# A two-layer encoder on one core: the second head pair's values in seven products, all values through memory, heads in four turns a chunk, and small moves at both ends

## The chip, the core and the metric

The kernel runs on one core of one Trainium2 chip. The metric is device time in microseconds (us) of one execution. Before the change three runs took 1619.01, 1621.74 and 1623.58 us, median 1621.74. The profiled execution, from which all rows below come, took 1620.87 us, of which the profile's span is 1619.1; the 1.8 us between them lie around the span.

## What is computed

The input is x, 512 tokens of width 2048 in float32. Two layers are added to it, each after an RMS norm, and a last RMS norm follows.

```python
def reference(x, norm_gain, final_gain, ...):
    for layer in range(2):
        hn = rmsnorm(x, norm_gain[layer])
        out = even_layer(hn, ...) if layer % 2 == 0 else odd_layer(hn, ...)
        x = x + out
    return rmsnorm(x, final_gain)

def odd_layer(h, w_in, gate_bias, norm_gain, w_out):
    proj = h @ w_in
    q, k, v, o, z, gates = split_at(proj, [1024, 1024, 2048, 2048, 2048, 32])
    # eight heads: q, k of 128 columns, v of 256; a forward and a backward mLSTM over chunks of 128 tokens
    h_f = mlstm_chunkwise(q, k, v, i_f, log_sigmoid(f_f))
    h_b = flip(mlstm_chunkwise(flip(q), flip(k), flip(v), flip(i_b), flip(log_sigmoid(f_b))))
    hs = rmsnorm(sigmoid(o) * (h_f + h_b), norm_gain)      # per head
    return (hs * silu(z)) @ w_out
```

The even layer is an attention of eight heads with two key and value heads beside a gated linear recurrence (RG-LRU), again between two large projections. The change lies in the odd layer, in the first chunk of the even layer's first projection, and in the final norm.

## The kernel before, in words

**Numbers.** Every float32 operand is split into a high and a low part (`split`, L152: ScalarE casts the high part, VectorE subtracts it to get the low one), and every product is made of three: high·high, high·low, low·high (`mm3`, L170). All matmuls are issued at L157, so rows of the profile are told apart by the names of the tiles.

**Bulk work.** The projections are a list of groups, each a block of weight columns in eight chunks of 256 rows, worked off by `run_steps` (L298). SP loads the chunk's weights (tile `raw`), `ahead` splits them early (`wh`, `wl`). There are two kinds of groups. A plain group has 512 columns in four PSUM banks and makes 192 matmuls of 512 moving columns (tile `bk`). A seven-product group adds and subtracts blocks of operands first (GpSimd sums weights into `w7s` and inputs into `ts`), so that seven block products do the work of eight; its matmuls have 256 moving columns (tile `s`). `run_w7c` works such a group of 512 columns: 8 chunks by 2 by 7 by 3, that is 336 matmuls. `run_w7` works one of 256 columns.

**Order of the odd layer.** Queries and keys; then `SC`, five seven-product groups of 512 columns: the values of head pair 0 (V0) and the gates O0 to O3; then the plain groups V1, V2, V3, Z3 and `out2` (the first 512 output columns); then five seven-product groups of 256 output columns (`u7`); then `run_last`, the last 256 output columns and the final norm.

**Heads.** The eight heads of the mLSTM (four pairs of two) and the transposition of their results (`hT_gen`) are generators in two lanes. While a plain group runs, lane 0 gets a turn after each bank listed in `TURNS`, so head work lies between bulk matmuls. `drain_until` runs a lane to its end where something later needs it: `h_split(c)`, which fetches the input chunk c of the output projection, needs that chunk stored by `hT_gen` (store to `hTd`, reload as `hTr`; the last pair's two chunks stay on chip as `hT`). A framework then orders each engine's instructions by their priorities and their dependences.

**Values.** V0 is scaled, stored to memory (`vd`) and reloaded (`vr`) by `v_gen`. V1 to V3 go straight from PSUM into the split tile `vv` (`v_evac`, L1174), which first drains the pair before (`need_h`).

**Both ends.** In the first chunk ScalarE writes the scaled high part `xh` (L527). At the end `acc` collects the squares of the output rows; `late_rows` (L1400) and `out2_square` (L1427) add to it, partly on GpSimd. `run_last` (L1439) makes two rows of blocks (`rows`), then two blocks of columns (`columns(0)`, `columns(1)`), each over 16 values of k. `next(between)` puts the row sums (`stc`, a matmul of ones with `acc`) and the spread reciprocal root (`rB`) among the columns' matmuls, at k = 1 and k = 5.

## Time and profile before

| What | us |
|---|---|
| runs, median (lowest to highest) | 1621.74 (1619.01 to 1623.58) |
| profiled execution, its span | 1620.87, 1619.1 |
| TensorE matmuls busy | 1598.5 (99% of the span) |
| VectorE, ScalarE, GpSimd busy | 1172.1, 881.8, 802.7 (72%, 54%, 50%) |
| five `SC` groups (963.70 to 1164.80) | 201.10 |
| last matmul to the end of the span | about 7 |

A timeline row gives start, duration, engine, line, operation, output and inputs, and in brackets the idle time of the engine ahead of it with what ended it. PE is TensorE, DVE is VectorE, ACT is ScalarE, POOL is GpSimd. [...] A row of a window gives the window, its length, the busy time of each engine with its count of instructions, the mean clock granted to TensorE (1.00 is full), the busy share of the DMA engines and their rate.

### The profile page before, as it was taken

To read this page: it belongs to the slowest core of one execution; us is meant where nothing else is said; L and a number is where in the kernel's file an instruction comes from. 1 tells how busy PE (TensorE), PEld (TensorE's weight loads), DVE (VectorE), ACT (ScalarE), POOL (GpSimd) and SP (SyncE) were. 2 spreads that over 40 slices of the span, in tenths; PEclk is the share of its full clock that TensorE was granted. 3 is DMA by queue.
4 is the path that set the end of the run, shared out by engine and by line. 5 is a ranking of instruction groups with operands and counts; after the bars stand their busy time and mean duration, and the time that the engine had idled before them with its cause. 6 is when DMAs were issued, how large, how long until landed. Compare 5 with 4: busy or idle time off the path is not lost.

```text
span 1619.1 us, 26278 instructions
## 1 busy us (share of the span) xinstructions
PE 1598.5 (99%) x9986; PEld 1431.9 (88%) x9986; DVE 1172.1 (72%) x1802; ACT 881.8 (54%) x1470; POOL 802.7 (50%) x804
## 2 busy tenths in 40 slices
PE   9999999999999999999999999999999999999997
PEld 7888888887888998889999999999988888888996
DVE  8755476766678786558998886666676676678875
ACT  6334666569584345544444444444566566565453
POOL 5220101101028884686787788888521322468862
PEclk9999999999999999999999999999999999999998
DMA  6533132431436358934444444444554344442564
GB/s 229 188 91 102 55 111 85 131 104 50 146 104 238 114 143 250 301 111 128 128 115 135 131 131 134 120 149 134 183 168 130 109 157 152 154 159 92 137 188 162
DMA packets 145486, 228.66 MB, mean 141 GB/s; under 512 B 10112, under 2 KB 70912, under 8 KB 145296
## 3 DMA queue, kind: packets, MB, share of 16 engines
q1 hardware_dynamic: 142000, 222.19, 43.6%
q0 software_dynamic: 2176, 4.19, 1.7%
q8 instruction: 78, 1.28, 0.3%
q10 hardware_dynamic: 1184, 0.60, 0.1%
q14 instruction: 48, 0.39, 0.1%
HBM read 189.17 MB, written 39.88 MB: 141 GB/s over the span
## 4 chain that ended last, share of the span: by engine, by line
PE 86%; DVE 4%; ACT 4%; POOL 2%; issue 2%; DMA 2%; SPq 0%; DVEq 0%; ACTq 0%; POOLq 0%
PE bk L157 41%; PE s L157 34%; DVE wl L154 2%; PE nf L157 2%; PE nb L157 2%; PE lg L157 1%; PE PV L157 1%; PE ST L157 1%; PE S L157 1%; PE tr L160 1%; ACT wh L153 1%; PE gt L157 0%; DMA hTr<-hTd 0%; DMA xres<-x2d 0%; DMA raw<-in_odd_w_out_dram 0%
## 5 line engine op out<-in xcount | busy, mean ns | idle before, releaser
L154 DVE TENSOR_TENSOR wl<-raw,wh 128x384 fp32r<-128x384 f32 (+3 forms) x349 | 365.4, 1049 | 185.0 <-ACT wh L153 184.3
L153 ACT CAST wh<-raw 128x384 fp32r<-128x384 f32 (+3 forms) x349 | 265.0, 762 | 378.8 <-PE s L157 274.9
L364 POOL TENSOR_TENSOR w7s<-raw 128x256 f32<-128x256 f32 x248 | 252.0, 1035 | 107.2 <-DMA raw<-in_odd_w_in_dram 61.4
L154 DVE TENSOR_TENSOR wl<-w7s,wh 128x512 fp32r<-128x512 f32 (+1 forms) x208 | 237.1, 1140 | 4.4 <-ACT wh L153 4.3
L157 PE MATMUL s<-th,wl 128*128 128x256 f32 x672 | 190.2, 283 | 0.8 <-DVE wl L154 0.8
L157 PE MATMUL s<-th,wh 128*128 128x256 f32 x672 | 189.1, 281 | 0.5 <-ACT wh L153 0.5
L157 PE MATMUL s<-tl,wh 128*128 128x256 f32 x672 | 189.2, 282 | 0.0
L157 PE MATMUL bk<-xh,wh 128*128 128x512 f32 x384 | 151.8, 395 | 0.0
L153 ACT CAST wh<-w7s 128x512 fp32r<-128x512 f32 (+1 forms) x208 | 145.3, 699 | 11.1 <-POOL w7s L364 9.5
L157 PE MATMUL bk<-xl,wh 128*128 128x512 f32 x384 | 151.3, 394 | 0.0
L157 PE MATMUL bk<-xh,wl 128*128 128x512 f32 x384 | 151.2, 394 | 0.0
L157 PE MATMUL s<-bh,wl 128*128 128x256 f32 x504 | 142.1, 282 | 1.1 <-DVE wl L154 1.1
L157 PE MATMUL s<-bh,wh 128*128 128x256 f32 x504 | 142.5, 283 | 0.6 <-ACT wh L153 0.6
L157 PE MATMUL s<-bl,wh 128*128 128x256 f32 x504 | 141.9, 282 | 0.0
L157 PE MATMUL bk<-bh,wh 128*128 128x512 f32 (+1 forms) x352 | 136.2, 387 | 0.0
L157 PE MATMUL bk<-bh,wl 128*128 128x512 f32 (+1 forms) x352 | 135.2, 384 | 0.0
L157 PE MATMUL bk<-bl,wh 128*128 128x512 f32 (+1 forms) x352 | 135.1, 384 | 0.0
L364 POOL TENSOR_TENSOR w7s<-w7s,raw 128x256 f32<-128x256 f32 x124 | 133.2, 1074 | 0.0
L157 PEld LDWEIGHTS s<-th,wl 128*128 128x128 f32 x672 | 127.0, 189 | 1.4 <-DVE wl L154 1.4
L157 PEld LDWEIGHTS s<-th,wh 128*128 128x128 f32 x672 | 127.1, 189 | 0.7 <-ACT wh L153 0.7
L157 PEld LDWEIGHTS s<-tl,wh 128*128 128x128 f32 x672 | 127.0, 189 | 0.0
L904 POOL TENSOR_TENSOR li<-li,xc 128x512 f32<-128x512 f32 x16 | 20.4, 1296 | 208.2 <-ACT li L896 208.2
(354 smaller groups left out, 4318.6 us busy)
## 6 DMA issues: line engine op xcount, KB each, us to landing
raw<-in_odd_w_in_dram SPq DMA_DIRECT2D x120, 512.0 KB, 3.9
raw<-in_even_w_in_dram SPq DMA_DIRECT2D x71, 512.0 KB, 3.8
raw<-in_even_w_out_dram SPq DMA_DIRECT2D x32, 512.0 KB, 4.1
raw<-in_odd_w_out_dram SPq DMA_DIRECT2D x32, 512.0 KB, 3.8
x2d<-x POOLq DMA_DIRECT2D x8, 512.0 KB, 6.1
xgd<-xg SPq DMA_DIRECT2D x8, 512.0 KB, 5.8
raw<-in_odd_w_in_dram SPq DMA_DIRECT2D x16, 256.0 KB, 4.3
xr<-xgd SPq DMA_DIRECT2D x8, 512.0 KB, 5.8
```

What stands on the lines that cost most here:

```text
L153: self.nc.scalar.copy(h, x)
L154: (eng or self.nc.vector).tensor_tensor(out=l, in0=x, in1=h.bitcast(F32), op=ALU.subtract)
L157: self.nc.tensor.matmul(out, a, b, start=start, stop=stop)
L160: self.nc.tensor.transpose(out, x, ident)
L364: po.tensor_tensor(out=s[:, :, q, :], in0=x, in1=y, op=op)
L904: nc.gpsimd.tensor_tensor(out=ii[j][:, d, :], in0=ii[j][:, d, :], in1=xc[:, j, :], op=ALU.mult)
```

## The change

It has seven parts. (1) V1 becomes a seven-product group in `SC`. (2) V2 and V3 are scaled and stored to `vd` like the others, and every pair's values come back through `v_load` and `v_gen`; the next pair's load is issued in the head before. (3) Lane 0 gets four turns a chunk. (4) In the first chunk VectorE writes `xh`, and the first step's matmuls run over all four banks for j = 0 before j = 1. (5) `out2` puts its scaling, squares and stores off (`later`), and the squares of rows 12 and 13, the last `u7` group's, are added on VectorE, not on GpSimd. (6) In the last `u7` group `late_rows` runs before a chunk's products, and its last call comes at the end of this group and no more in `run_last`. (7) In `columns(0)` the row sums stand at k = 5 and the spread at k = 13, in `columns(1)` at k = 1 and k = 9.

```diff
-O7, V7 = (0, 1, 2, 3), (0,)
-TURNS = (0, 1, 2)
-STD = 'V1 V2 V3'
+O7, V7 = (0, 1, 2, 3), (0, 1)
+TURNS = (0, 1, 2, 3)
+STD = 'V2 V3'
...
-                    self.bulk_mm(g, g["ps"][b], g["x"](c), ws, b, c)
+                    self.bulk_mm(g, g["ps"][b], g["x"](c), ws, b, c, (0, 1) if i else (0,))
...
+                if i == 0:
+                    for b in range(4):
+                        self.bulk_mm(g, g["ps"][b], g["x"](c), ws, b, c, (1,))
...
+            if g.get("each"):
+                g["each"](c)
             for n in range(7):
                 product(n, c)
...
-            if g.get("each"):
-                g["each"](c)
...
-            nc.scalar.activation(h[:, j, :], raw[:, j, :], AF.Copy, scale=gcol)
+            if c:
+                nc.scalar.activation(h[:, j, :], raw[:, j, :], AF.Copy, scale=gcol)
+            else:
+                nc.vector.tensor_scalar(out=h[:, j, :], in0=raw[:, j, :], scalar1=gcol, scalar2=None, op0=ALU.mult)
...
+    def v_load(self, p):
+        self.vq[p] = [self.slot2("vr") for _ in range(2)]
+        for u in range(2):
+            self.nc.sync.dma_start(out=self.vq[p][u], in_=self.vd[p, u])
+
     def v_gen(self, p):
-        for u in range(2):
-            x = self.slot2("vr")
-            nc.sync.dma_start(out=x, in_=self.vd[p, u])
+        if p not in self.vq:
+            self.v_load(p)
+            yield
+            yield
+        for u, x in enumerate(self.vq.pop(p)):
...
     def v_evac(self, p):
         def f(tt, ps):
-            if p > 0:
-                self.need_h(p - 1)
-            t = self.v_tile(p, tt)
-            nc.scalar.activation(t[:, 0, :, 0:256], v2, AF.Copy, scale=r)
-            nc.vector.scalar_tensor_tensor(out=t[:, 1, :, 0:256], in0=v2, scalar=r,
+            t, u = tt // 2, tt % 2
+            if t == 0:
+                self.vx[u] = self.slot2("vx")
+            self.nc.scalar.activation(self.vx[u][:, t, :], ps, AF.Copy, scale=self.r2[:, tt:tt + 1])
+            if t:
+                self.nc.sync.dma_start(out=self.vd[p, u], in_=self.vx.pop(u))
...
                 self.head_load(p + e, 1 - e)
+                if e and (p + 1, 0) in self.vd:
+                    self.v_load(p + 1)
...
         self.nc.vector.tensor_add(x3, x3, ps)
+        self.later.append(partial(self.out2_rest, b))
+
+    def out2_rest(self, b):
         self.out2_scale(b)
...
-            (self.nc.gpsimd if 4 <= k < 14 else self.nc.vector).tensor_tensor(
+            self.nc.vector.tensor_tensor(
...
-                if k in (1, 5):
+                if k in ((1, 9) if u else (5, 13)):
                     next(between)
...
-        self.late_rows(5)
...
             def f():
+                add(0, self.v_gen(p))
                 add(0, self.head_gen(p, 0))
...
-            if 2 <= c <= 4 or c == 7:
-                self.x3_load({2: 2, 3: 3, 4: 4, 7: 5}[c])
+            if c in (2, 3, 4, 6):
+                self.x3_load({2: 2, 3: 3, 4: 4, 6: 5}[c])
             if c >= 5:
                 self.late_rows(c - 3)
+            if c == 7:
+                self.later.append(partial(self.late_rows, 5))
```

Three places show how this moves instructions. The first is the start of the program. On VectorE there stood before (`wl` and `wh` are the parts of weights, `xl` and `xh` those of the input, `xr` its raw form):

```order
L154 TENSOR_TENSOR wl_133<-raw_119,wh_132 128x512 x2
L528 SCALAR_TENSOR_TENSOR xl_135<-xr_118,pb,xh_134 128x512 x2
L528 SCALAR_TENSOR_TENSOR xl_150<-xr_124,pb,xh_149 128x512 x2
L154 TENSOR_TENSOR wl_160<-raw_126,wh_159 128x1024
L528 SCALAR_TENSOR_TENSOR xl_168<-xr_128,pb,xh_167 128x512 x2
```

On VectorE there stands now:

```order
L154 TENSOR_TENSOR wl_133<-raw_119,wh_132 128x512 x2
L533 TENSOR_SCALAR xh_134<-xr_118,pb 128x512 x2
L534 SCALAR_TENSOR_TENSOR xl_135<-xr_118,pb,xh_134 128x512 x2
L534 SCALAR_TENSOR_TENSOR xl_150<-xr_124,pb,xh_149 128x512 x2
L154 TENSOR_TENSOR wl_160<-raw_126,wh_159 128x1024
L534 SCALAR_TENSOR_TENSOR xl_168<-xr_128,pb,xh_167 128x512 x2
```

Two instructions that write `xh_134` have come to VectorE between the weights' low parts and the input's. On ScalarE there stood before, after the same chunk's two casts of weights:

```order
L527 ACTIVATE xh_134<-xr_118,pb 128x512 x2
L527 ACTIVATE xh_149<-xr_124,pb 128x512
L567 ACTIVATE xr_118<-xr_118 128x512 x2
L527 ACTIVATE xh_149<-xr_124,pb 128x512
L567 ACTIVATE xr_124<-xr_124 128x512
L153 CAST wh_159<-raw_126 128x1024
L567 ACTIVATE xr_124<-xr_124 128x512
```

On ScalarE there stands now:

```order
L531 ACTIVATE xh_149<-xr_124,pb 128x512 x2
L573 ACTIVATE xr_118<-xr_118 128x512 x2
L573 ACTIVATE xr_124<-xr_124 128x512 x2
L153 CAST wh_159<-raw_126 128x1024
L531 ACTIVATE xh_167<-xr_128,pb 128x512 x2
```

The cast of the second chunk's weights (`wh_159`) now stands behind all four squares of the two input chunks, which are made in place and so come after VectorE has read `xr`.

The second place is the end of the last head. On TensorE its last matmuls (`nf`, `nb`) were followed before by the bulk of Z3 (`bk`), of which 90 matmuls stood ahead of the first transposition of the last pair's result (`hT2223`):

```order
L157 MATMUL nb2163_14798<-vv2035_14102,wB2112_14496 128x258 x2
L157 MATMUL nb2163_14798<-vv2035_14102,wB2113_14497 128x258
L157 MATMUL bk2061_14211<-bh952_5946,wh2118_14525 128x512
L157 MATMUL bk2061_14211<-bl953_5947,wh2118_14525 128x512
L157 MATMUL bk2061_14211<-bh952_5946,wl2119_14526 128x512
```

Now the head ends inside `out2`, the transpositions of pair 2 (`hT2232`, `hT2241`) follow it at once, and 26 bulk matmuls stand between them and the first transposition of the last pair (`hT2266`):

```order
L157 MATMUL nb2227_15174<-vv2093_14494,wB2173_14888 128x258 x2
L157 MATMUL nb2227_15174<-vv2093_14494,wB2174_14889 128x258
L160 MATMUL hT2232_15205<-ident_87,hfb2001_13951 128x128 x2
L160 MATMUL hT2232_15205<-ident_87,hfb2002_13952 128x128 x2
L160 MATMUL hT2241_15243<-ident_87,hfb2001_13951 128x128 x2
L160 MATMUL hT2241_15243<-ident_87,hfb2002_13952 128x128 x2
L157 MATMUL bk2217_15105<-bl2157_14805,wh2187_14947 128x512
```

From the last transposition to the first `s` of the `u7` groups there are 108 bulk matmuls in both. On ScalarE, before, the last head's result (`hfb2071`, `hfb2072`) was scaled by the head's norm (`rh`) behind the reload of chunk 3 (`hTr2187`):

```order
L153 CAST bh2188_14907<-hTr2187_14905 128x2x2x256
L1215 ACTIVATE hfb2071_14263<-hfb2071_14263,rh2175_14864 128x256
L153 CAST th2191_14916<-ts2169_14838 128x1024
L1215 ACTIVATE hfb2071_14263<-hfb2071_14263,rh2175_14864 128x256 x3
L1215 ACTIVATE hfb2072_14264<-hfb2072_14264,rh2175_14864 128x256 x4
```

Now the scaling (of `hfb2122`, `hfb2123`) stands behind the reload of chunk 4 (`hTr2233`), and the evacuation of the last pair's transpositions (`hT2265`) behind that of chunk 5 (`hTr2249`):

```order
L153 CAST bh2234_15214<-hTr2233_15212 128x2x2x256
L1225 ACTIVATE hfb2122_14645<-hfb2122_14645,rh2243_15264 128x256
L153 CAST th2237_15223<-ts2200_15029 128x1024
L1225 ACTIVATE hfb2122_14645<-hfb2122_14645,rh2243_15264 128x256 x3
L1225 ACTIVATE hfb2123_14646<-hfb2123_14646,rh2243_15264 128x256 x4
L153 CAST wh2286_15439<-raw2264_15341 128x1024
L153 CAST bh2250_15277<-hTr2249_15275 128x2x2x256
L153 CAST th2253_15286<-ts2236_15218 128x1024
L1257 ACTIVATE hT2265_15351<-hT2266_15352,pb_88 128x512
```

The third place is VectorE at the end. Before, the squares of the late rows were added to `acc` (L1407) after the last `u7` group's results had been added (L1391), and ahead of the additions that follow the rows of `run_last` (L1424):

```order
L1391 TENSOR_TENSOR xres2378_16316<-xres2378_16316,x72418_16624 128x512 x2
L1407 TENSOR_TENSOR acc32256_15290<-acc32256_15290,sq32431_16662 128x256 x2
L1424 TENSOR_TENSOR xres2412_16585<-xres2412_16585,bk2433_16672 128x256
L1424 TENSOR_TENSOR xres2412_16585<-xres2412_16585,bk2434_16673 128x256
L1435 TENSOR_TENSOR acc32256_15290<-acc32256_15290,sq32435_16771 128x256
```

Now in that place stand the squares of rows 12 and 13 (L1450), which GpSimd added before:

```order
L154 TENSOR_TENSOR wl2471_16943<-raw2469_16940,wh2470_16942 128x1024
L500 TENSOR_TENSOR x72462_16914<-x72462_16914,s72429_16640 128x256
L501 TENSOR_TENSOR x72462_16914<-x72462_16914,s72429_16640 128x256
L1406 TENSOR_TENSOR xres2420_16596<-xres2420_16596,x72462_16914 128x512 x2
L1450 TENSOR_TENSOR acc32308_15617<-acc32308_15617,sq32464_16925 128x512
L1450 TENSOR_TENSOR acc32308_15617<-acc32308_15617,sq32465_16930 128x512
L1439 TENSOR_TENSOR xres2455_16867<-xres2455_16867,bk2475_16952 128x256
```

and the last late row's squares (`sq32460`, L1422) have gone ahead, among the splits of the weights of `run_last`:

```order
L154 TENSOR_TENSOR wl2448_16798<-raw2443_16766,wh2447_16797 128x1024
L1422 TENSOR_TENSOR acc32308_15617<-acc32308_15617,sq32458_16873 128x256 x2
L1422 TENSOR_TENSOR acc32308_15617<-acc32308_15617,sq32460_16904 128x256 x2
L154 TENSOR_TENSOR wl2457_16870<-raw2451_16832,wh2456_16869 128x1024
L154 TENSOR_TENSOR wl2468_16937<-raw2466_16934,wh2467_16936 128x1024
```

So `wh2456` and `wl2457`, the second of the four weight splits that `run_last` reads, now come after work that waits for reloaded rows.

More of the change, by code (lines that the diff above doesn't have):

```diff
@@ L273, in first_split, with bulk_mm @@
         self.wsp[0] = (wh, wl)
-    def bulk_mm(self, g, ps, xs, ws, b, c):
+    def bulk_mm(self, g, ps, xs, ws, b, c, js=(0, 1)):
         (xh, xl), (wh, wl) = xs, ws
         f = slice(b * P, (b + 1) * P)
-        for j in range(2):
+        for j in js:
             st = c == 0 and j == 0
@@ L1155, in v7_evac @@
         return evac
+    def v_load(self, p):
+        self.vq[p] = [self.slot2("vr") for _ in range(2)]
+        for u in range(2):
+            self.nc.sync.dma_start(out=self.vq[p][u], in_=self.vd[p, u])
     def v_gen(self, p):
-        nc = self.nc
-        for u in range(2):
-            x = self.slot2("vr")
-            nc.sync.dma_start(out=x, in_=self.vd[p, u])
+        if p not in self.vq:
[3 more added lines that the diff above has]
+        for u, x in enumerate(self.vq.pop(p)):
             for th in range(2):
@@ L1164, in v_gen @@
                 self.split(t[:, 0, :, 0:256], t[:, 1, :, 0:256], x[:, th, :].rearrange("p (h d) -> p h d", h=2))
-        yield
+            yield
     def v_tile(self, p, tt):
@@ L1175, in f @@
         def f(tt, ps):
-            nc = self.nc
-            if p > 0:
-                self.need_h(p - 1)
-            t = self.v_tile(p, tt)
-            r = self.r2[:, tt:tt + 1]
-            v2 = ps.rearrange("p (h d) -> p h d", h=2)
-            nc.scalar.activation(t[:, 0, :, 0:256], v2, AF.Copy, scale=r)
-            nc.vector.scalar_tensor_tensor(out=t[:, 1, :, 0:256], in0=v2, scalar=r,
-                                           in1=t[:, 0, :, 0:256].bitcast(F32), op0=ALU.mult, op1=ALU.subtract)
+            t, u = tt // 2, tt % 2
[3 more added lines that the diff above has]
+            if t:
+                self.vd[p, u] = self.dp.tile([P, 2, S], F32, tag=f"vd{p}{u}", name=f"vd{p}{u}")
+                self.nc.sync.dma_start(out=self.vd[p, u], in_=self.vx.pop(u))
         return f
@@ L1564, in build @@
         self.zTd = self.dp.tile([D, S], F32, tag="zTd", name="zTd")
-        self.h3, self.z3, self.og, self.vd, self.hl, self.x3d = {}, {}, {}, {}, {}, {}
+        self.h3, self.z3, self.og, self.vd, self.hl, self.x3d, self.vq, self.vx = ({} for _ in range(8))
         self.xgd = self.dp.tile([D, S], F32, tag="xgd", name="xgd")
```

## The prediction

> **What bounds the kernel now.** I read the page's busy times first.
>
> ```profile
> PE 1598.5 (99%) x9986; PEld 1431.9 (88%) x9986; DVE 1172.1 (72%) x1802; ACT 881.8 (54%) x1470; POOL 802.7 (50%) x804
> ```
>
> TensorE is the bound: 99% busy. Time can go in three ways: fewer or shorter matmuls, fewer waits of TensorE, less of what lies ahead of the first and behind the last matmul. Next, what TensorE waited for, over the whole span (us in all, times, longest):
>
> ```profile
> PE stc L157 <- DVE acc L1435: 2.5, 1, 2.5
> PE s L157 <- DVE wl L154: 2.4, 5, 0.8
> ```
>
> The longest single wait is that of the row sums (`stc`) at the end. The rest are small and stand in three places, which I took one by one by windows: the start, the stretch around the last head and the first `u7` group, and the end.
>
> ```profile
> 963.70:1164.80 201.10, 200.13 (x1684) 199.04 (x1683) 135.77 (x152) 91.08 (x113) 164.34 (x160) 1.00 0.46 139
> 1164.80:1400.00 235.20, 235.20 (x1234) 200.01 (x1233) 162.58 (x391) 151.50 (x344) 53.97 (x74) 1.00 0.46 144
> 1400.00:1520.00 120.00, 117.40 (x706) 103.62 (x705) 93.41 (x129) 67.72 (x119) 89.34 (x84) 0.99 0.44 136
> 1476.30:1495.00 18.70, 17.00 (x125) 16.20 (x124) 17.30 (x23) 11.29 (x21) 13.07 (x15) 0.91 0.47 163
> 1590.80:1602.70 11.90, 9.41 (x66) 9.19 (x65) 6.77 (x25) 3.63 (x8) 4.24 (x5) 0.86 0.01 1
> 1595.00:1600.00 5.00, 5.00 (x31) 5.00 (x32) 2.60 (x15) 0.00 (x0) 0.00 (x0) 0.66 0.01 3
> ```
>
> The first row is `SC`, the second the plain groups with the heads: there TensorE has no idle time at all. The third loses 120.00 − 117.40 = 2.6 us to waits, and the fourth shows the clock granted at 0.91 over 18.7 us, so another 18.7 × 0.09 = 1.7: together 4.3 us around the last head. The last two show the same at the end.
>
> **Part 1, V1 in seven products.** The pace of plain bulk and of seven-product bulk, from the chain of waits:
>
> ```profile
> 115.90 5.55 PE bk L157 x24
> 543.38 79.63 PE s L157 x672
> ```
>
> A plain group has 192 matmuls at 5.55/24 = 0.231 us: 44.4. By the first of the windows above five `SC` groups take 201.10, so 40.2 each (336 matmuls at 79.63/672 = 0.118 would be 39.8). V1 moves from one kind to the other: **−4.2** (−3.7 to −4.6 by these two rates). GpSimd's sums for it lie beside the group, as for the others (164.34 of 201.10 us busy); its store and reload replace an evacuation.
>
> **Parts 2 and 3, values through memory and four turns.** The heads' matmuls stay the same in number; they only lie closer. By the order's counts and the paces above, a head begins about every 31.8 us before and 27.5 after. If all that VectorE and ScalarE do in the second window were head work, their shares 162.58/235.20 = 69% and 151.50/235.20 = 64% would rise by 31.8/27.5 to 80% and 74%. Neither becomes the bound. I take **+0.3** for short waits (0 to +3, three waits like the 0.91 of `nb` below). The store and reload of V2 and V3 lie beside bulk work, the reload being issued one head ahead, 27 us against the 9 that store and reload take below; with that cover gone it would cost up to 9 for a pair.
>
> **Part 4, the first chunk.**
>
> ```profile
> 7.90 0.50 PE L157 MATMUL bk<-wh,xh 128*128 128x512 f32 x1 [1.03 <-ACT xh L527]
> 14.64 0.50 PE L157 MATMUL bk<-wl,xh 128*128 128x512 f32 x1 [0.65 <-DVE wl L154]
> 7.26 0.69 DVE L154 TENSOR_TENSOR wl<-raw,wh 128x512 fp32r<-128x512 f32 x1 [1.55 <-ACT wh L153]
> 11.16 1.04 ACT L153 CAST wh<-raw 128x1024 fp32r<-128x1024 f32 x1
> 12.28 2.31 DVE L154 TENSOR_TENSOR wl<-raw,wh 128x1024 fp32r<-128x1024 f32 x1
> L1094 DVE TENSOR_SCALAR gF<-gM x1: 410/410/410, 821.9 to 821.9; 64x512 f32<-64x512 f32 x1
> L881 DVE TENSOR_SCALAR lr<-lg,pb x16: 739/751/754, 165.3 to 455.1; 128x512 f32<-128x512 f32 x16
> ```
>
> TensorE begins at 7.90 on ScalarE's `xh`, and after 25 matmuls waits for the second chunk's `wl` until 14.64. Now VectorE makes `xh` after both `wl` (from 7.95). The new instruction isn't in the trace at this size from this memory: 0.41 us (half the partitions) and 0.75 (read from PSUM) bound it at t. After the two come four `xl` (0.69 each, like the `wl` of their size), a square on ScalarE (0.52, half a cast's width), the cast of the second weights (1.04, now behind all squares) and `wl` (2.31), with 0.05 at each of four handoffs (`wl` ended at 14.59, the matmul began at 14.64): 7.95 + 2t + 2.76 + 0.52 + 1.04 + 2.31 + 0.2 = 14.8 + 2t, or 15.8 at t = 0.5. By the new order 27 matmuls are done by then, not 25, worth 0.46. So 15.8 − 14.64 − 0.46 = **+0.7**: between +0.5 and +1.2 by t, and −0.6 if this `wl` is not slowed, for elsewhere one of the same size took 1.23:
>
> ```profile
> 1585.92 1.23 DVE L154 TENSOR_TENSOR wl<-raw,wh 128x1024 fp32r<-128x1024 f32 x1 [0.30 <-ACT wh L153]
> ```
>
> [...]
>
> **Around the last head.**
>
> ```profile
> 1422.31 0.62 PE L157 MATMUL nb<-vv,wB 128*128 128x258 f32 x3 [0.91 <-ACT hT L1247]
> 1430.37 1.28 ACT L1227 ACT_TABLE_LOAD   x1
> 1431.66 1.16 ACT L1227 ACTIVATE z<-z 128x512 f32<-128x512 f32 x2
> 1437.94 2.91 ACT L1215 ACTIVATE hfb<-hfb,rh 128x256 f32<-128x256 f32 x7
> 1445.35 0.74 POOL L550 TENSOR_TENSOR ts<-hTr 128x256 f32<-128x256 f32 x1 [11.64 <-DMA hTr<-hTd]
> 1469.08 1.44 POOL L364 TENSOR_TENSOR w7s<-raw 128x256 f32<-128x256 f32 x2
> 1476.26 0.29 PE L157 MATMUL s<-bh,wh 128*128 128x256 f32 x1
> hTd<-hT SPq DMA_DIRECT2D x6, 512.0 KB, 3.8
> hTr<-hTd SPq DMA_DIRECT2D x6, 512.0 KB, 5.4
> ```
>
> Before, the last head's matmuls end at 1422.9 and its scaling on ScalarE at 1440.9: 18 us, covered by 90 bulk matmuls (20.8). After, the cover is 26 (6.0 us, and 0.9 of transpositions). The chain is shorter, since the gating of z (a table load and two pairs, 1.28 + 2 × 1.16 = 3.6 us of ScalarE) and some four casts (1.04 each) now stand elsewhere: about 10.2. That leaves a new wait of some 3.3 us at the first transposition, 1 to 7 by how early the reload of chunk 4 lands (3.8 + 5.4 us after its store is ready).
>
> The wait of before comes from GpSimd: four chunks of `ts` from 1445.35, then `w7s` from 1469.08, 7.2 us ahead of the first `s`, too late by 2.6 us. After, `ts` can begin some 8 us behind the last head (one round trip), takes about 21 (the 23.7 from 1445.35 to 1469.08 less its waits), so `w7s` begins at about 29, and `s` without a wait could begin at 29 + 7.2 + 2.6 = 39. TensorE has 146 bulk matmuls and the transpositions, 34.9 us. So about 4.1 us are lost in all, of which the 3.3 are a part, and 0.7 for a lower clock that need not come: 4.8 against 4.3, **+0.5** (−4.3 if the waits go, +9.8 in the slow rival below).
>
> **The end.**
>
> ```profile
> 1589.22 2.65 POOL L1435 TENSOR_TENSOR acc<-acc,sq 128x512 f32<-128x512 f32 x2 [8.67 <-ACT sq L1433]
> 1594.63 0.35 PE L157 MATMUL stc<-ones,acc 128*128 128x2 f32 x2 [2.49 <-DVE acc L1435]
> 1598.26 0.49 DVE L601 TENSOR_SCALAR diag<-ident,r 128x128 f32<-128x128 f32 x2
> 1595.65 4.45 PE bk L157 x24
> 1600.66 6.10 PE bk L157 x51
> 1605.00:1607.00 2.00, 2.00 (x20) 2.00 (x19) 1.27 (x6) 0.00 (x0) 0.00 (x0) 1.00 1.03 344
> 1613.00:1615.00 2.00, 0.00 (x0) 0.00 (x0) 1.23 (x4) 0.00 (x0) 0.94 (x2) 0.50 0.56 177
> ```
>
> `columns(0)` takes 11.9 us. In it TensorE waits 2.5 for `acc`, whose chain passes GpSimd's 2.65, and then runs 24 matmuls in 4.45, where the next 51 take 0.120 each: 4.45 − 2.87 = 1.6 lost to the clock. After, the two additions of GpSimd are on VectorE, and the sums stand at k = 5, 1.8 us of matmuls and the identity's 0.6 later; the chain (two additions, a square, an addition) fits into that. The spread at k = 13 stands 8 × 0.355 = 2.8 and the sums' 0.9 behind it, its chain took 3.6 to 4.1 (from `stc` at 1594.63 to the end of `diag` at 1598.75). Gone: 2.5 + 1.6 = 4.1. What is late next is the output: the first half's stores now start 1.6 us nearer to the end, and the DMA engines are full from 1603 (1.03 at 1605), with about 1 us to spare at 1613. I give back 0.5: **−3.6** (−4.1 to −0.5, if `acc` is still late by 2 and the clock falls).
>
> A price stands against it. The second weight split of `run_last` now comes behind the squares of row block 5:
>
> ```profile
> x2d<-x POOLq DMA_DIRECT2D x1, 512.0 KB, 10.4
> xres<-x2d SPq DMA_DIRECT2D x5, 512.0 KB, 8.4
> 1565.10 1.21 POOL L959 DMA_DIRECT2D x2d<-x  x1
> 1575.60 0.36 SPq L1398 DMA_DIRECT2D xres<-x2d  x1
> ```
>
> That block is stored at 1565.1, landed after 10.4, and was reloaded from 1575.6. The split is needed at about 1582.3 (rows begin 11.4 ahead of 1590.8, and k = 4 is 2.85 later). With 8.4 for the reload and 2.9 for square, cast and split TensorE would wait 4.6. But one 512 KB load no longer runs against the store, which is 1.6 us at the 344 GB/s above, and the reload is first in its queue: with 5.4, as for `hTr`, it ends at 1582.3. I take **+0.8** (0 to 4.6). Two weight loads queue behind it on SP; they were issued at 1576 before, and are issued no later now.
>
> **Sum.** −4.2 − 3.6 + 0.8 + 0.7 + 0.5 + 0.3 = −5.5. Against the profiled execution's 1620.87 (span 1619.1 and 1.8 around it) that is 1615.4. The median of the runs is 0.9 above it, within their spread.
>
> **Rivals.**
> - *The last head's wait comes on top.* The 3.3 at the transposition and 1.7 of lower clock are paid, and the wait at the first `s` stays: +5.0 instead of +0.5, 1619.9. For it: the cover falls from 90 to 26 matmuls; against: TensorE held up early gives GpSimd time. Chance 0.15.
> - *Slower.* Both reloads (chunks 4 and 5) stand on ScalarE ahead of the last pair's scaling and evacuation, two round trips of 9.2 us in a row. Less the cover of 6.0 that is 12.4, with 1.7 of clock 14.1, and the old wait stays: −6.0 + 14.1 = +8.1, 1629.0. It decides once the zone loses more than 11.7 us over before (1626.6, which is 0.3% slower, less 1614.9). Against it: the two transfers can run side by side. Chance 0.06.
> - *The zone's waits vanish and the start costs nothing*: −5.5 − 4.8 − 0.7 = −11.0, 1609.9. Chance 0.14.
> - *The end's wait only moves*, to `run_last`'s second split: +4.6 instead of +0.8, 1619.2. Chance 0.12.
> - *The low clock at the end isn't due to the wait*: then 1.6 stay, 1617.0. What speaks against it is that it follows that wait at once. Chance 0.04. [...]
>
> **How the numbers follow.** The forecast, 1615.4, holds 0.49, from 1611 to 1619. A difference of 0.3%, 4.9 us, is about what a measurement of this kernel can tell from none, so faster means below 1616.9. Of the 0.49, 0.36 lie below it; with the third rival and bits of the others faster gets 0.54, same 0.39, slower 0.07. The range reaches from the third rival to beyond the first: 1609 to 1622.5.
>
> **What would show it.** In the changed kernel's profile: `SC` with six groups in about 241 us; the first matmul after 8.3 and the second chunk's `wl` ending near 15.5; a wait of 2 to 5 us at the last pair's `hT`, and less than before at the first `s`; no wait over 0.5 at `stc`, no low clock behind it and `columns(0)` in 8 us; a wait of about 1 us inside the rows of `run_last`. I am wrong if TensorE idles in the dense head stretch, or if the second split waits long for row block 5.

## The result, and the profile after

The changed kernel is slower. Its four runs took 1643.72 to 1649.09 us, median 1645.99, beside 1622.03 (1619.01 to 1623.58) for the kernel before: a ratio of 1.0156, with a 95% interval of 1.0143 to 1.0169 (estimated from all runs; the two medians alone give 1.0148). One of the four runs of e3 below, and one of seven of the kernel before on the chip of e11 to e15, took about twice as long or more (3192 and 4056 us), and both are left out of all that follows. The forecast was 1615.4, and the time lies above the whole range. The profiled execution took 1647.46 us with a span of 1645.6, that is 26.5 us more span than before. The busy times of the page (busy time, share of the span, instructions of each engine):

```profile
PE 1605.5 (98%) x10130; PEld 1438.8 (87%) x10130; DVE 1191.3 (72%) x1828; ACT 892.6 (54%) x1489; POOL 824.0 (50%) x834
```

TensorE has the 336 − 192 = 144 more matmuls of a seven-product group, and no other engine's share has risen. Nothing in this line tells of the loss. It shows when the odd layer is cut at its groups. The windows of the kernel after for `SC`, V2, V3, Z3 and `out2` (columns as before: window, length, busy us of PE, PEld, DVE, ACT and POOL, clock, DMA share, GB/s):

```profile
965.50:1208.60 243.10, 241.33 (x2022) 239.17 (x2021) 159.66 (x179) 108.05 (x133) 188.61 (x191) 1.00 0.44 132
1208.60:1276.50 67.90, 67.79 (x348) 56.29 (x347) 52.53 (x131) 46.61 (x107) 14.90 (x22) 1.00 0.57 187
1276.50:1358.20 81.70, 76.11 (x401) 64.36 (x400) 52.63 (x131) 53.81 (x126) 22.11 (x27) 0.96 0.53 165
1358.20:1446.50 88.30, 76.58 (x397) 63.86 (x395) 65.64 (x142) 55.54 (x124) 34.93 (x40) 0.96 0.52 165
1446.50:1508.20 61.70, 57.55 (x271) 47.08 (x271) 40.58 (x63) 36.14 (x66) 40.23 (x38) 0.94 0.26 88
```

The same groups before, V2, V3, Z3 and `out2`:

```profile
1229.80:1295.50 65.70, 65.70 (x348) 56.06 (x347) 42.66 (x105) 39.25 (x92) 15.11 (x22) 1.00 0.41 126
1295.50:1360.90 65.40, 65.40 (x348) 55.84 (x346) 45.97 (x113) 40.35 (x95) 14.33 (x22) 1.00 0.47 147
1360.90:1429.90 69.00, 68.09 (x368) 57.77 (x366) 48.21 (x103) 44.60 (x99) 33.77 (x31) 1.00 0.49 155
1429.90:1476.00 46.10, 46.10 (x207) 37.61 (x208) 34.31 (x37) 27.61 (x40) 31.52 (x28) 1.00 0.36 115
```

Before, TensorE is busy all through V2, V3 and `out2` at full clock. After, from V3 on, it idles in every group and the clock falls with it (0.96, 0.96 and 0.94). More matmuls in a longer window are no loss by themselves, so I compare with the pace: for every two neighbouring matmuls in the trace, the time between their starts beyond 0.231 us (512 moving columns), 0.1185 (256), 0.1195 (258) or 0.065 (my estimate for the small ones, too low: before, four transpositions `hT` from 1277.86 took 0.35 to the next start, 0.088 each; with that the totals of both kernels are 1.5 lower). I take starts and not durations, since rows overlap: before, a row of 512 columns at 1239.82 lasts 0.39, and the next starts at 1240.05. The sum over a group, called **lost** below, holds waits and low clock alike. It is 1.5, 10.3, 16.9 and 9.7 us in the four groups after, 38.4 in all. Before, it is 0.7, 0.6, 0.5, 2.8 and 1.0 in the five groups V1 to `out2`, 5.6 in all. So these groups lose 32.8 us more, which is more than the whole difference: V2 and V3 11.8 after (1.1 before), Z3 and `out2` 26.6 (3.8 before). The rest of the 26.5: +1.8 up to `SC`; 42.0 for V1 (243.10 − 201.10) in place of 44.4, −2.4; and from the end of `out2` to the end of the span 1645.6 − 1508.2 = 137.4 us instead of 1619.1 − 1476.0 = 143.1, −5.7. 1.8 − 2.4 + 32.8 − 5.7 = 26.5.

What TensorE waited for in that stretch (1140 to 1520; total us, times, longest):

```profile
PE nb L157 <- DVE dd L1324: 6.2, 1, 6.2
PE ST L157 <- ACT k L153: 5.8, 3, 3.2
PE hT L160 <- ACT hfb L1225: 4.2, 1, 4.2
PE ST L157 <- DVE q L154: 4.1, 3, 1.4
```

Only the 4.2 at `hT` is a wait that the prediction had. The other three are of a kind that the kernel before does not have: a head's first matmuls (`ST`) wait until their queries and keys have been split, and the eighth head's `nb` waits for its decay matrix (`dd`). Ahead of the fifth head's first `ST` TensorE was idle from 1327.45 to 1330.66. That matmul, and ScalarE's timeline ahead of it:

```profile
1330.66 0.50 PE L157 MATMUL ST<-q,k 128*128 128x512 f32 x1 [3.21 <-ACT k L153]
...
1324.91 0.42 ACT L1214 ACTIVATE hsq<-hfb 128x256 f32<-128x256 f32 x1 [1.35 <-POOL hfb L1359]
...
1327.55 0.42 ACT L1214 ACTIVATE hsq<-hfb 128x256 f32<-128x256 f32 x1 [1.37 <-POOL hfb L1359]
...
1327.97 1.03 ACT L153 CAST wh<-raw 128x1024 fp32r<-128x1024 f32 x1
1328.90 0.68 ACT L1257 ACTIVATE hT<-hT,pb 128x512 f32<-128x512 f32 x1
1329.48 0.61 ACT L153 CAST q<-qkr 128x512 fp32r<-128x512 f32 x1
1329.99 0.62 ACT L153 CAST k<-qkr 128x512 fp32r<-128x512 f32 x1
```

ScalarE is idle twice, for 1.35 and 1.37 us, and while it is idle the casts of `q` and `k` stand ready behind: their loads were issued at 1305 and had landed by 1309.4. In these rows ScalarE kept to the order of its queue, and that queue holds the end of the head before. One piece of that end goes `nf` (TensorE), `hfb` (ScalarE), `hfb` (VectorE), `hfb` (GpSimd), `hsq` (ScalarE), and both times ScalarE waits for GpSimd's part. Here the next head could not start until this chain had run out. The eighth head's `nb`, and VectorE's timeline ahead of it:

```profile
1444.81 0.99 PE L157 MATMUL nb<-vv,wA 128*128 128x258 f32 x3 [6.19 <-DVE dd L1324]
...
1439.47 0.94 DVE L154 TENSOR_TENSOR wC<-dd,wC 128x256 fp32r<-128x256 f32 x1
...
1440.65 1.43 DVE L154 TENSOR_TENSOR bl<-hTr,bh 128x1024 fp32r<-128x1024 f32 x1
1442.00 1.74 DVE L154 TENSOR_TENSOR tl<-ts,th 128x1024 fp32r<-128x1024 f32 x1
1443.67 0.47 DVE L1322 SCALAR_TENSOR_TENSOR dd<-ST,r2s,dd 128x256 f32<-128x256 f32 x1
1444.06 0.60 DVE L1324 SCALAR_TENSOR_TENSOR dd<-ST,r2s,dd 128x384 f32<-128x384 f32 x1
```

The last `dd` stands behind two wide splits (`bl`, `tl`) that belong to the output projection's input, 3.2 us of work for a later group, about half of the wait. TensorE ran nothing else in its 6.19 us: the matmuls just ahead of `nb` in its own queue were the head's, and the bulk stood behind (from 1446.45).

### The profile page after: what moved, and what is told of

Its sections match the earlier page's. It is cut to its first block, busy times and chain, and to the rows that moved or that the text cites. A ratio compares the mean times of both kernels' runs of the same rounds, so it can differ in the third digit from the quotient of the medians.

```text
span 1645.6 us, 26690 instructions
## 1 busy us (share of the span) xinstructions
PE 1605.5 (98%) x10130; PEld 1438.8 (87%) x10130; DVE 1191.3 (72%) x1828; ACT 892.6 (54%) x1489; POOL 824.0 (50%) x834
## 3 DMA queue, kind: packets, MB, share of 16 engines
q1 hardware_dynamic: 143728, 228.48, 44.1%
## 5 line engine op out<-in xcount | busy, mean ns | idle before, releaser
L154 DVE TENSOR_TENSOR wl<-raw,wh 128x384 fp32r<-128x384 f32 (+3 forms) x349 | 372.3, 1069 | 197.0 <-ACT wh L153 195.4
L367 POOL TENSOR_TENSOR w7s<-raw 128x256 f32<-128x256 f32 x264 | 264.1, 1024 | 123.8 <-DMA raw<-in_odd_w_in_dram 64.0
L154 DVE TENSOR_TENSOR wl<-w7s,wh 128x512 fp32r<-128x512 f32 (+1 forms) x216 | 242.5, 1123 | 7.1 <-ACT wh L153 7.1
L153 ACT CAST wh<-w7s 128x512 fp32r<-128x512 f32 (+1 forms) x216 | 153.7, 712 | 17.7 <-POOL w7s L367 16.0
L367 POOL TENSOR_TENSOR w7s<-w7s,raw 128x256 f32<-128x256 f32 x132 | 139.7, 1058 | 0.0
L367 POOL TENSOR_TENSOR w7s<-raw,w7s 128x256 f32<-128x256 f32 x132 | 125.3, 949 | 9.7
```

The lines of the kernel that those rows point to most:

```text
L153: self.nc.scalar.copy(h, x)
L154: (eng or self.nc.vector).tensor_tensor(out=l, in0=x, in1=h.bitcast(F32), op=ALU.subtract)
L367: po.tensor_tensor(out=s[:, :, q, :], in0=x, in1=y, op=op)
```

## The experiments

The theories, with the letters that the expectations use. **D**: the heads lie too close; a head's chain through the engines needs more bulk matmuls between two heads than it gets. **M**: values through memory cost the time, by their reloads, splits and the pauses around them. **O**: the last heads lie among the output projection's input splits and reloads. **P**: `q` and `k` are split too late, and more room ahead of `ST` would mend it. **S**: the pool of memory slots (`NSLOT`) is too small for the values on the way. **Room** (in e20): eight heads need five plain groups, whatever way the values take.

Two numbers describe a kernel's order, counted in its trace: the bulk matmuls between the first `ST` of one head and of the next (**pitch**; before 84 and 108 in turn, after 78; the first and the last head can differ), and the bulk matmuls left in Z3 and `out2` behind the last head's last one (**left**; before 222, after 146). "Lost" is given for the groups in which heads lie and `out2`. Ratios, with 95% intervals, are to the kernel before on the same chip, estimated from all runs as above, so they differ a little from the quotient of two medians.

| kernel | median us | ratio | pitch | left | lost in V1, V2, V3, Z3, out2 |
|---|---|---|---|---|---|
| before | 1620.15 to 1622.03 | | 84/108 | 222 | 0.7, 0.6, 0.5, 2.8, 1.0 |
| after | 1645.99 | 1.0156 (1.0143 to 1.0169) | 78 | 146 | –, 1.5, 10.3, 16.9, 9.7 |
| e4_ends_only | 1617.28 | 0.9978 (0.9969 to 0.9987) | 84/108 | 222 | 0.8, 0.6, 0.5, 2.8, 1.0 |
| e1_before_four_turns | 1628.19 | 1.0041 (1.0025 to 1.0057) | 66/126 | 258 | 1.5, 0.9, 0.8, 8.8, 2.0 |
| e2_changed_v1_plain | 1624.17 | 1.0016 (1.0005 to 1.0026) | 66/126 | 234 | 2.1, 3.1, 1.7, 6.9, 0.8 |
| e3_changed_three_turns | 1660.78 | 1.0239 (1.0213 to 1.0265) | 90/108, last 23 | 96 | –, 0.4, 0.4, 8.1, 36.0 |
| e5_v1_seven_alone | 1640.33 (one run) | | 30 to 90 | 222 | –, 16.2, 2.1, 7.5, 3.2 |
| e6_values_memory_alone | 1633.95 | 1.0084 (1.0069 to 1.0099) | 84 to 132 | 148 | 0.9, 0.4, 1.2, 13.0, 7.8 |
| e11_wider | 1658.73 | 1.0234 (1.0218 to 1.0251) | 78/102 | 96 | –, 1.3, 2.5, 13.9, 28.4 |
| e13_narrower | 1637.73 | 1.0110 (1.0094 to 1.0126) | 60 to 84 | 204 | –, 2.1, 9.6, 11.9, 2.3 |
| e12_split_later | 1649.04 | 1.0182 (1.0164 to 1.0200) | 78 | 146 | –, 2.1, 9.8, 16.1, 11.8 |
| e18_turn_moved | 1653.82 | 1.0205 (1.0189 to 1.0220) | 78 | 109 | –, 1.3, 10.1, 16.1, 13.1 |
| e15_fewer_slots | 1691.78 (one run) | | 78 | 146 | –, 3.7, 8.5, 16.7, 8.9 |
| e9_o0_plain_no_pause | 1636.12 | 1.0099 (1.0084 to 1.0114) | 78 | 338 | 2.7, 7.2, 2.4, 13.5, 1.7 |
| e10_o0_plain_wider | 1630.41 | 1.0064 (1.0047 to 1.0080) | 78/102 | 264 | 1.0, 0.4, 2.1, 14.1, 2.1 |
| e20_o0_plain_three_turns | 1642.93 | 1.0143 (1.0126 to 1.0160) | 90/114 | 228 | 0.7, 0.2, 1.4, 24.4, 2.9 |

In the last three the five groups are V2, V3, O0, Z3 and `out2`.

**The two ends alone.** e4 is the kernel before with parts 4 to 7 of the change and without parts 1 to 3. Its edit against the changed kernel (what takes `v_load`, `v_gen` and `v_evac` back is left out):

```diff
-O7, V7 = (0, 1, 2, 3), (0, 1)
-TURNS = (0, 1, 2, 3)
-STD = 'V2 V3'
+O7, V7 = (0, 1, 2, 3), (0,)
+TURNS = (0, 1, 2)
+STD = 'V1 V2 V3'
...
-                add(0, self.v_gen(p))
```

> The kernel before with parts 4 to 7 of the change alone (first chunk, putting off out2's scaling, the late rows, the sums and spreads in the columns), V1 plain, values straight from PSUM, three turns. All theories: the end gains 3 to 4 us, the start loses 0.6, the rows of the last group 0.6: 1617 to 1621 us.

It takes 2.9 us less than before (1617.28 beside 1620.15; the interval of the ratio ends at 0.9987) as expected, and is the fastest of all kernels here, though by 0.22% at the ratio, less than the 0.3% that the prediction took for its bound. So the whole loss sits in parts 1 to 3.

**One part of the three at a time.** e1 is the kernel before with four turns and nothing else. e2 is the changed kernel with V1 plain again, e3 the changed kernel with three turns. The three edits, in this order (e1 against the kernel before, e2 and e3 against the changed one):

```diff
-TURNS = (0, 1, 2)
+TURNS = (0, 1, 2, 3)
...
-O7, V7 = (0, 1, 2, 3), (0, 1)
-STD = 'V2 V3'
+O7, V7 = (0, 1, 2, 3), (0,)
+STD = 'V1 V2 V3'
...
-TURNS = (0, 1, 2, 3)
+TURNS = (0, 1, 2)
```

> The kernel before with four turns a chunk instead of three, nothing else. By the order a head follows the other head of its pair after 25 us instead of 30 and then waits 40 us for the next pair's values, so a pair still takes 65 us. D (heads too dense: a head's chain over ScalarE, VectorE and GpSimd is longer than the room between heads that follow without a pause): 1622 to 1627 us, small waits inside a pair. M (values through memory cost at each change of pair): 1622, no such wait. O (the last head ends among the splits of the output projection's inputs): 1620 to 1622, since the last head ends 9 us of bulk earlier.

> The changed kernel with V1 as a plain group again (V1, V2, V3 plain, all values through memory, four turns, both ends as changed). The pause of 40 us between pairs is back, the last head ends inside Z3. D: nearly all waits of the head stretch go, 1620 to 1627 us. M: the waits at the changes of pair stay, about 12 us: 1631 to 1636. O: only the last 20 us of waits go, 1629 to 1633 (1646 - 20 + 4.2 for V1).

> The changed kernel with three turns a chunk. By the order heads begin 27 to 36 us apart, the last two pairs run later, and the last head is driven through in 15 us inside the output projection. D: the waits at the third and fourth pair's starts (some 13 us) shrink to under 5, but the last head's grow: 1640 to 1650. M: waits at the changes of pair stay, 1646 to 1655. O: the loss at the last head grows, 1646 to 1660.

Four turns alone cost 8.0 us (1628.19 − 1620.15), more than any expectation for e1, most of it in Z3 (8.8 lost, 2.8 before). That is one wait of 6.4 us at the end of Z3, told below; no wait of a head is longer than 0.5. Four turns with values through memory and the ends' moves, but with V1 plain, cost 4.0 (6.9 without the 2.9 that e4 gains), as D alone had said. With V1 gone from the plain groups, giving up the fourth turn is worse, not better: V2 and V3 then lose 0.4 each, less than before, but the last head lies in `out2` and that group loses 36.0. Its time lies above what D (1640 to 1650) and M had said, and 0.8 us above O's range; the place is O's. So a wide pitch saves the groups that host heads and pays at their end.

e5 is e4 with V1 in seven products (`V7 = (0, 1)`, `STD = 'V2 V3'`), where V2 and V3 still go straight from PSUM. e6 is e2 with three turns: values through memory with the old density of turns.

> The kernel before with both ends as changed (1617.3 us) and, of the head parts, part 1 alone: V1 in seven products, V2 and V3 straight from PSUM, three turns. V2 must drain pair 1 before its evacuation, so by the order heads 3 to 6 follow after 17 to 26 us. All theories of dense heads: 1640 to 1670 us. If the seven products themselves cost the time, as much as the changed kernel: 1644.

> The kernel before with both ends as changed (1617.3 us) and, of the head parts, part 2 alone: all values through memory, V1 plain, three turns. D (dense heads): within 2 us of 1617.3, since heads stay 29 to 40 us apart; the four turns then made all of the 6.9 us by which the kernel with V1 plain and four turns lay above 1617.3. M (values through memory): the 6.9 stay, 1622 to 1625.

In e5 the values of a pair may not overwrite those of the pair before, so the heads are run to their ends at the end of V2: pitches of 30 to 61, and V2 loses 16.2. Without part 2, part 1 pays at another place, but by this one run no more: e5 lies 5.7 us below the changed kernel. e6 missed both its expectations, 1617 and 1622 to 1625. In it V1, V2 and V3 lose 2.5 in all, about as much as before, so M as the cost of reloads and splits falls. But a pair's heads wait for its values to be made, stored and reloaded (pitches up to 132), so the last head comes late (148 left) and Z3 and `out2` lose 20.8. The changed kernel has no such pauses: its pitch stays near 78.

The medians of these kernels, all with both ends as changed, also price the parts. Taking V1 out of the plain groups costs 22 to 27 us whatever else is in: e4 to e5 +23.0, e6 to e3 +26.8, e2 to after +21.8. Values through memory alone cost 16.7 (e4 to e6), and four turns on top of them win back 9.8 with V1 plain (e6 to e2) and 14.8 without (e3 to after). So part 1, which was to save 4.2 us, makes most of the loss.

**Density.** e9 is the changed kernel with five plain groups again: O0 is plain in place of V1 (`O7 = (1, 2, 3)`, `STD = 'V2 V3 O0'`). It has after's pitch without its late end. e10 is e9, and e11 the changed kernel, with two more turns between the split of `q` and `k` and the first `ST`; e13 is the changed kernel with one turn less behind `ST`; e18 moves one from there to ahead of `ST`; e20 is e9 with `TURNS = (0, 1, 2)`. The edits of e9, of e10 and e11, and of e13, all against the changed kernel (e10 has the first two):

```diff
-O7, V7 = (0, 1, 2, 3), (0, 1)
-STD = 'V2 V3'
+O7, V7 = (1, 2, 3), (0, 1)
+STD = 'V2 V3 O0'
...
             self.split(t[:, 0, :], t[:, 1, :], raw[:, w, :])
         yield
+        yield
+        yield
         wA = [self.slot("wA", F32R) for _ in range(2)]
...
         if e == 0:
             self.hfb[p] = [self.slot2("hfb") for _ in range(2)]
         yield
-        yield
         for i in range(NT):
```

> The changed kernel with the gate group O0 plain (after V3) in place of seven products: V0 and V1 in seven products, all values through memory, four turns. Five plain groups as before, but heads follow without a pause every 28 us, as in the changed kernel, and the last ends in Z3, ahead of the output projection. Bulk work as with V1 plain. O (the loss comes from the last heads lying among the splits and reloads of the output projection's inputs): 1617 to 1622. D (heads without a pause every 28 us fall behind): the waits from the fifth head on stay, 10 to 20 us: 1627 to 1640.

> The same with two more turns between a head's q, k and its first product, so that by the order heads are 28 and 34 us apart and the last still ends in Z3. D: 5 us or more faster than without the extra turns, 1617 to 1625. O: the same as without them, within 2 us. P (TensorE waits because it stands in a fixed order behind too late q, k): the waits at the first products (ST) go, others stay.

> The changed kernel with two more turns between a head's q, k and its first product: by the order heads begin 28 and 34 us apart instead of 28, and the last head's last matmul comes 11 us of bulk later, deeper in the output projection. In the changed kernel TensorE loses 1.5, 10.3, 16.9 and 9.7 us in V2, V3, Z3 and the first output group. D (dense heads alone): V3's loss falls under 3 and Z3's too, 1628 to 1636 us. D and O (also heads beside the splits of the output projection's inputs): V3 under 3, but Z3 and the output group together lose 27 or more, 1638 to 1650. O alone: V3 stays near 10, 1650 to 1665.

> The changed kernel with one turn fewer between a head's weights and its value products: by the order heads begin 24 to 27 us apart (one gap of 30) and the last head's last matmul comes 14 us of bulk earlier. D: V2 and V3 lose 15 or more (11.8 in the changed kernel), total 1648 to 1660. O: Z3 and the output group lose 10 us less than 26.6, 1633 to 1638. D and O: both, 1640 to 1650.

> The changed kernel with one of the two turns behind a head's ST products moved to between its q, k splits and ST; heads still begin 28 us apart and end at the same place. P (q and k are only too late): V3's loss of 10.3 us falls under 4, total 1634 to 1641. D (the head's whole chain is too long for 28 us): the wait moves to nf and nb, V3 loses 7 or more, total 1642 to 1652.

> The changed kernel with O0 plain after V3 in place of seven products and three turns a chunk: V0 and V1 in seven products, all values through memory, no pause between pairs, heads 27 to 37 us apart by the order as in the kernel before, last head's end within 3 us of bulk of where it was before. Room (heads need five host groups, whatever way the values take): V2, V3 lose under 2 us each, total 1616 to 1622. M (values through memory): V2 and V3 lose 5 or more each, 1627 or more.

The loss of V3 follows the pitch, as D says. From 78 to 78/102 it falls from 10.3 to 2.5 in e11 and from 7.2 to 0.4 in e10, and with 90 or more it is 0.2 (e20) and 0.4 (e3). The mean seems to count more than the smallest: with 66 and 126 in turn (e1, e2; mean 96) V2 and V3 lose 0.8 to 3.1 each. V3 of e11:

```profile
1273.60:1341.20 67.60, 66.36 (x350) 56.33 (x348) 49.19 (x117) 44.16 (x103) 16.82 (x22) 1.00 0.49 152
```

It is 14 us shorter than after's (81.70), at full clock; 51 matmuls less lie in it, so 7.8 of the 14 is lost time. P falls: in e18, with the same pitch, V3 loses 10.1, where P had said under 4; the gap ahead of the fifth head's first `ST` is smaller (1.95 us beyond the pace, 3.37 in after), and others at `nb`, `nf` and `nb` have grown or come (1.3, 1.26 and 0.82). In e13, against D, a narrower pitch than 78 loses no more: V2 and V3 lose 11.7 together (11.8 in after), where D had said 15 or more. Why is not shown. Density is not all of it either: in O0 of e9 three heads lie at a pitch of 66 to 78 and lose only 2.4, where V3 before it lost 7.2. The reason is open.

What e11 won in V3 (7.8) it lost more than twice over in `out2` (18.7 more), so that its time lies 9 us above what D and O together had said. Its last head lies there and is run to its end at once, with no bulk matmuls between its parts. The window of `out2` and the timeline of TensorE in e11:

```profile
1423.40:1515.20 91.80, 77.94 (x356) 63.66 (x357) 58.42 (x116) 52.37 (x109) 39.19 (x37) 0.84 0.25 81
```

```profile
1462.06 0.39 PE L157 MATMUL nf<-vv,wA 128*128 128x258 f32 x1 [0.83 <-DVE wA L154]
1463.34 0.99 PE L157 MATMUL nb<-vv,wA 128*128 128x258 f32 x3 [0.90 <-DVE den L1354]
1465.77 1.41 PE L157 MATMUL nf<-vv,wA 128*128 128x258 f32 x5 [0.79 <-DVE dd L1326]
1468.99 1.02 PE L157 MATMUL nb<-vv,wC 128*128 128x258 f32 x3 [0.95 <-DVE dd L1326]
1473.08 1.66 PE L157 MATMUL nf<-vv,wA 128*128 128x258 f32 x6 [1.14 <-ACT hfb L1358]
```

Each link of the head's chain is now a wait of TensorE, with a 7.0 us wait at `hT` behind it and a clock of 0.84 over the group. In the kernels that differ from after only in the heads' turns, the loss of Z3 and `out2` together rises as the bulk left falls: 14.2 with 204 left (e13), 26.6 with 146 (after), 29.2 with 109 (e18), 42.3 with 96 (e11) and 44.1 with 96 (e3). e13 met O's expectation in both its numbers, and at 1637.73 is 8.3 us faster than the changed kernel. This is O, as far as five kernels show it: each head that moves also changes what lies around it. It is why both kernels with a wider pitch in four plain groups (e3, e11) lose more than they win.

The three kernels with O0 plain have five plain groups again, and none came near the time of before. e9 lies in D's range, but by luck: D expected 10 to 20 us of waits from the fifth head on, and 11 of the 13.5 us that Z3 lost are another wait. e10 is 5.7 us faster than e9, as D said, and still 5 us above D's range. e20 had neither fault by these two numbers, and yet lies more than 20 us above its expectation (Room). V2, V3 and O0 lost 2.3 together, as expected, but Z3 lost 24.4. The same shows in e9. TensorE, ScalarE and VectorE in e9's timeline:

```profile
1452.83 0.77 PE L157 MATMUL bk<-bh,wh 128*128 128x512 f32 x1 [10.92 <-DVE z L1236]
...
1437.96 1.05 ACT L153 CAST bh<-hTr 128x1024 fp32r<-128x1024 f32 x1 [6.74 <-DMA hTr<-hTd]
...
1452.00 2.47 DVE L1236 TENSOR_TENSOR z<-bk,rB 128x512 f32<-128x512 f32 x4
```

The first bank of `out2` waits until VectorE has emptied Z3's banks (`z`), and VectorE's emptying stands behind the input splits, which wait for reloads. This one wait is 6.4 us in e1, 10.9 in e9, 7.9 in e10, 15.8 in e20, 2.7 in e11 and 1.0 in e13, and is absent from before and after. I read it from the trace; no kernel was made that takes it away alone, and what makes it long in one kernel and short in another stays open.

**When the input is fetched, and the slots.** e12 calls `h_split` one chunk later. e15 sets `NSLOT = 35` instead of 37.

```diff
         def early2(c):
-            if c == NCH - 1:
-                h_next()
+            pass
...
         def late2(c):
-            if c < NCH - 1:
-                h_next()
+            h_next()
```

> The changed kernel with the inputs of the output projection fetched and split one chunk (5.6 us of bulk) later each. Heads as in the changed kernel. D: no change, within 3 us of 1646. O: Z3 loses 5 or more us less, 1632 to 1641, unless the later reload is then itself waited for in the output group (its loss over 9.7).

> The changed kernel with 35 instead of 37 slots of the shared pool that holds heads, values, inputs and rows. S (the pool is short, and loads and casts wait for a slot): 10 us slower or more, 1656 and up. D and O: within 4 us of 1646.

e12 loses as much as after and in the same groups (16.1 and 11.8), where O had expected 5 us less in Z3: the splits `bl` and `tl` of the next chunk stand ahead of the last `dd` again, and `nb` waits 5.8 for it. So a chunk's shift does not free the heads; the splits still lie among them, so it does not tell D and O apart. e15 (one run) is 46 us slower, as S had said by the total, but not here: V2 to `out2` lose 37.8, as after's 38.4. About 26 us come before V2 and 19 behind `out2`. The loss in these groups does not answer to two slots less, so S is not seen in it; a larger pool was not tried.

## Why the prediction was wrong, point by point

- **V1 in seven products: right in sign, too high.** −4.2 was forecast, with `SC` in about 241 us. It took 243.1, so in its own group V1 saved 2.4 where −3.7 was my smallest (a figure that follows from neither of the two rates named for it). The mis-sized term is the length of a group: six at 40.5 us (243.10/6), where five had taken 40.2 each.
- **Parts 2 and 3: the step that failed.** It said that a head begins every 27.5 us instead of 31.8, that VectorE's and ScalarE's shares would rise to 80% and 74%, "neither becomes the bound", and so +0.3 (0 to +3). Indeed neither became the bound: over V2, V3 and Z3 VectorE was busy (52.53 + 52.63 + 65.64)/237.9 = 72% and ScalarE 66%; without the 28.7 us lost there the shares are 82% and 75%, much as forecast. Yet V1 to `out2` lost 32.8 us more than before, and the shares did not tell it. A head is a chain that crosses four engines again and again, and in the rows above it stands in the order of a queue: the casts of `q` and `k` behind ScalarE's waits of 1.35 and 1.37 us, the last `dd` behind 3.2 us of VectorE's splits. What the step left out is how much bulk has to lie over that chain. In its own terms, "they only lie closer" was put at +0.3; V2 and V3 alone lost 11.8 us (1.1 before), and a wider pitch brought V3 from 10.3 to 2.5 (e11). The row that should have warned was in the window that I read: 235.20 us, TensorE busy 235.20. I took it as room; it was the state in which 84 and 108 bulk matmuls covered the chain.
- **Around the last head: +0.5 forecast.** The step's own wait came (4.2 at `hT`, 3.3 forecast, 2 to 5 named as the sign), and the wait at the first `s` went, as said. What it missed is that the last heads moved into the stretch where the output projection's inputs are reloaded and split: the eighth began 90 bulk matmuls into Z3's 192 before, and 178 after. It counted the cover behind the last head, not the cover inside it: Z3 lost 16.9 us, most of it at `ST` and `nb`. The sum also took a round trip at 8 us, where its rows, and the rival, say 9.2; with 9.2 the term would have been +1.7, still far too small.
- **The rivals** named a loss in the zone of at most 14.1 us, from the two reloads. None named the heads' own chain. My last sentence did ("if TensorE idles in the dense head stretch"), with no chance and no price.
- **The start: right.** +0.7 forecast.

The timeline of the start, after:

```profile
8.77 0.47 PE L157 MATMUL bk<-wh,xh 128*128 128x512 f32 x1 [1.23 <-DVE xh L533]
15.69 0.51 PE L157 MATMUL bk<-wl,xh 128*128 128x512 f32 x1 [0.41 <-DVE wl L154]
8.14 0.88 DVE L533 TENSOR_SCALAR xh<-xr,pb 128x512 fp32r<-128x512 f32 x2
```

The second chunk's `wl` is ready 1.05 us later than before, with two more matmuls done (0.46): +0.6. The new operation takes 0.44 us, so t lay near the row of 0.41. Within the sum two misses cancel: the four `xl` took 3.09 us, not 2.76, and `wl` 1.97, not 2.31. That the total is so close is partly luck. The rest of the 1.8 us up to `SC` comes later and was not followed.

- **The end: right.** No wait at `stc`, no low clock, and `columns(0)` in 8.2 us (8 forecast). The window and the timeline of TensorE, after:

```profile
1618.80:1627.00 8.20, 8.20 (x69) 8.03 (x68) 5.78 (x23) 3.22 (x6) 0.00 (x0) 1.00 0.01 2
```

```profile
1614.29 0.38 PE L157 MATMUL bk<-bh,wl 128*128 128x256 f32 x1 [0.34 <-DVE wl L154]
1622.59 0.33 PE L157 MATMUL stc<-ones,acc 128*128 128x2 f32 x2
1626.73 0.70 PE L157 MATMUL rB<-diag,ones 128*128 128x256 f32 x2
```

The wait in the rows of `run_last`, forecast as 0.8, is two of about 0.3. The forecast of this wait took 1.6 us for 512 KB at 344 GB/s, which is 1.5; it changes nothing. e4 tests both ends together: −2.9 us measured, where −3.6 + 0.8 + 0.7 = −2.1 had been said.

So the one step outweighs all others: seven-product groups host no heads, so moving V1 among them saved 2.4 us of matmuls and took away one of five groups, 192 bulk matmuls, from under eight heads. In V2, V3 and Z3 there are 576. Eight heads at the pitch that lost nothing (84 and 108, mean 96) want 768, which is what V1, V2, V3 and Z3 gave before. With V1 plain again the changed kernel takes 1624.17 us instead of 1645.99 (e2). That the cover is all of it is not shown: e10 and e20 have 768 again, with O0 in V1's place, and lost most of their time at the wait for Z3's banks.

## What to carry to other kernels

Work that is hidden beside bulk matmuls needs a count of cover, not a share: take the bulk matmuls between two starts of the hidden chain in the kernel that loses nothing, and ask whether the changed order still has that number for every one of them, the last included. The count is needed and not enough: e20 had it and lost 24.4 us in one group to another wait. Before a cheaper form of some bulk is used, see what it was covering. And a window in which the bound engine is 100% busy tells only that the cover is enough, not by how much.

## What was not expected of the hardware

- **The clock fell behind waits of 1.35 and 1.28 us, and not behind 1.19 and 1.42.** Between 1320 and 1350 of the kernel after, TensorE was idle for 4.6 us (30.00 − 25.40), nearly all of it in two pieces at `ST` (3.21 and 1.38), and the granted clock over the window was 0.89:

```profile
1320.00:1350.00 30.00, 25.40 (x118) 20.53 (x117) 21.14 (x53) 20.87 (x52) 6.86 (x9) 0.89 0.34 106
```

So V3 lost more than it waited: its waits add up to 5.6 us, its loss, low clock included, is 10.3. The clock was low behind shorter waits too: the seventh head's `ST` waited 1.35 us until 1394.41 and 1.28 until 1396.20, and the clock fell to half (0.50). The eighth head's `ST` waited 1.19 and 1.42 us, until 1429.85 and 1432.46, and it stayed at full (1.00). The windows behind the two pairs:

```profile
1396.00:1398.00 2.00, 1.80 (x5) 1.31 (x6) 1.44 (x6) 0.90 (x2) 0.00 (x0) 0.50 0.01 5
1433.00:1435.00 2.00, 2.00 (x10) 1.60 (x9) 1.02 (x3) 0.44 (x1) 0.00 (x0) 1.00 0.82 213
```

- **VectorE's splits of one size took different times.** A split of 128x1024 took 1.23 us at 1585.92 before, 1.43 (`bl`) and 1.74 (`tl`) in the rows at 1440.65 and 1442.00 after, and 2.31 at 12.28 before. What made the difference was not tried.
